# Four dense expert tiles instead of five, with two tiles of the first part gathered early into five row buffers

## The chip, the cores and the metric

The kernel runs on one core of one Trainium2 chip. The metric is the device time of one execution in microseconds. A core has TensorE (PE; its weight loads are listed as PEld), VectorE (DVE), ScalarE (ACT), GpSimd (POOL), SyncE (SP, which issues plain DMAs here) and 16 DMA engines that all queues share.

## The reference

One layer of a decoder trunk for 1024 prompt tokens and 32 sample tokens (8 requests of 4), model width 1024, in float32: a mixing block (dilated window attention in 8 heads beside a gated linear recurrence in 4 heads), a cross attention to 256 memory tokens, a PEER feed-forward block, and a final norm. The feed-forward block is what the change is about. For every token, 8 heads choose 16 of 16384 single-neuron experts:

```python
e = (take_along_axis(i1, ci // 16) * 128 + take_along_axis(i2, ci % 16))   # expert numbers, 8 x 16 per token
g = softmax(sc)
u = peer_u[e]                                      # rows of 1024 floats
a = gelu(einsum('td,thkd->thk', x, u))
y = einsum('thk,thkd->td', g * a, peer_v[e])
```

The outputs are the normed rows of all tokens, the new keys, values and recurrent states, and the memory keys and values.

## The kernel before

**Tiles and parts.** The tokens make nine tiles: 0 to 7 are 128 prompt tokens each, 8 is the 32 sample tokens. Everything up to the choice of experts is done in three parts (`PARTS`, line 24): tiles 0, 1, 2, then 3, 4 and the sample, then 5, 6, 7. A part has a `middle` (projection, attention, recurrence, line 505) and a `tail` (output projection, cross attention, scores of the 128 x 128 product keys, and `select_tile`, line 924, which finds the 16 experts of each head). `run` (line 1211) interleaves generators by weights: the middle of one part beside the tail of the part before (lines 1239 to 1244). The projections use three matmuls for one product (line 202 to 204: high x high, high x low, low x high), since every operand is split into a rounded part and a rest.

**Two ways through the experts.** A tile in `DENSE` (line 25) is computed against all 16384 experts by matmuls. For it `gates` (line 993) first builds a table of gate values, expert by token, out of one-hot comparisons (lines 1013, 1018, or 1021 and 1022 on ACT) and small matmuls (line 1024), and stores it to DRAM (`gtall`, line 1030, 8 MiB for a tile). `LATE` gives for each dense tile how many of four comparisons go to ACT. The gates of the first `NG` dense tiles run beside the second part's tail, the others beside the third part's tail. Then `dense` (line 1034) goes through 128 steps, each with 128 experts: it loads a block of `u` (line 1070) and of `v` (line 1072), 512 KB each, splits both into two halves (lines 170, 171), multiplies all dense tokens with `u` (lines 202 to 204, tile `a`; before in two halves of 320 tokens), applies Gelu (line 1082), multiplies by the gates (line 1084), splits again, and adds the product with `v` (lines 1092 to 1094). `KG = (3, 4)`: three tiles accumulate in PSUM throughout (`y`), the others are added up every fourth step in `yr` and SBUF (`ys`, line 1121).

Any other tile is gathered (`gather_tile`, line 1159): for each of its 128 expert slots (32 for the sample, which is spread over the partitions) an indirect DMA fetches 128 rows of `peer_u`, 512 KB, one row for each token (line 1177, on POOL's queue), and one VectorE instruction forms 128 dot products (line 1184). After Gelu and gates, as many rows of `peer_v` are fetched and added up by line 1195. So a whole tile takes 256 gathers and the sample 64. Each fetch needs a row buffer of 4 KB in every partition: `g_row` (line 1153) has two in the pool `gat`; once `EARLY` = 90 gathers are written down in the program, three in each five come from the pool `more`, which opens in the dense stage, when the selections of the last part are done and `late` is closed (line 1253). The two buffers of `gat` also serve as staging for gates (`BIG`, line 1007). Tile `ha` (the tokens, then the sum), `ix`, `gw` and `dots` exist once, so a tile's loads wait for the tile before.

**Order.** The program is handed to a scheduler that orders each engine's instructions beforehand by a timeline of its own and by the program's order; gathers come last in the program, so they fill gaps. On the chip each queue then runs in that fixed order. The selections of tiles 5, 6, 7 are put off into the dense stage (`picks`, line 703). Gathered are, in this order, the tiles 8, 7, 6, 5 (line 1258), 832 gathers in all. GpSimd writes the descriptors of indirect DMAs into an area of SBUF whose size is an argument of `Bacc` (line 1356; 16384 bytes of each partition if not given).

Of the kernel before, what the change touches and what calls it, by code (L numbers as in the profile page):

```python
# [8 lines left out]
F32 = mybir.dt.float32  # L9
# [11 lines left out]
D = 1024  # L21
EPS = 1e-6
NEG = -1e30
PARTS = ((0, 1, 2), (3, 4, 8), (5, 6, 7))
DENSE = (0, 1, 2, 3, 4)
NG = sum(t in PARTS[0] for t in DENSE)
GT = 16

# [5 lines left out]
VS = 1  # L34
XA = (16, 1)
GA = (10, 1)
EARLY = 90
KG = (3, 4)
VS2 = 1
LATE = (0,0,2,2,2)  # L40
MR = 3
LB = 3
RAW = 1
BIG = 1
W0 = (1,1)
W1 = (2,1,1)
W2 = (2,1,1)
# [18 lines left out]
def _body(tc, nc, ctx, A, O):  # L66
# [24 lines left out]
    def T(p, shape, dt=F32, tag=None, bufs=None):  # L91
        seq[0] += 1
        kw = {} if bufs is None else {"bufs": bufs}
        if p is wk:
            p = wl if tag in LONG else wr if tag == "res" else we
        return p.tile(shape, dt, name=f"{tag}_{seq[0]}", tag=tag, **kw)
# [72 lines left out]
    def split(hi, lo, src):  # L169
        S.copy(hi, src)  # L170
        V.tensor_tensor(lo, src, hi, op=ALU.subtract)  # L171
# [862 lines left out]
    def dense(dv, dn, dps):  # L1034
# [28 lines left out]
        def hidden(i, out):  # L1063
            if i == 0:
                for h in (1, 0):
                    for r in range(4):
                        gate_piece(0, h, r)
            k, h = divmod(i // 4 + 2, 2)
            gate_piece(k, 1 - h, i % 4)
            uhl = load_split(dn, [128, 8, 128], A["uT"][i], "u", 5)  # L1070
            u = [[y[:, 4 * j : 4 * j + 4] for y in uhl] for j in range(2)]
            vhi, vlo = load_split(dv, [128, D], vrow[i], "v", 11)
            ga = T(dv, [128, M], F32, "w", 11)
            whi, wlo = (T(dv, [128, M], F32R, "w", 11) for j in range(2))
            out.extend((whi, wlo, vhi, vlo))
            for h in range(2):
                lo, hi = h * (M // 2), (h + 1) * (M // 2)
                kg, ki = divmod(i + 4 * h, 8)
                ki -= 4 * h if kg == 0 else 0
                pa = T(dps, [128, 512], F32, "a", 6 - 2 * KEEP + 1 if KEEP > 2 else 2)[:, : M // 2]  # L1080
                mm3(pa, u, x, 8, slice(lo, hi))
                S.activation(ga[:, lo:hi], pa, AF.Gelu)  # L1082
                gv = ga[:, lo:hi].rearrange("p (b t) -> p b t", t=GT)
                V.tensor_tensor(gv, gv, gts[kg, h][:, :, ki], op=ALU.mult)  # L1084
                split(whi[:, lo:hi], wlo[:, lo:hi], ga[:, lo:hi])
                yield

        def product(o, t, dh, ws, start, stop):
            sl = slice(t * 128, (t + 1) * 128)
# [11 lines left out]
        for i in range(128):  # L1101
# [9 lines left out]
                del kept[:n]  # L1111

            next(ahead, None)
            keep(KEEP - 1)
            next(ahead, None)
            for t, dh in sums:
                keep(1)
                ds = slice(dh * 512, (dh + 1) * 512)
                o = T(dps, [128, 512], F32, "yr", 1 if KEEP > 2 else 2)
                product(o, t, dh, hist[done[t] :], True, True)  # L1120
                V.tensor_tensor(ys[t - KEEP][:, ds], ys[t - KEEP][:, ds], o, op=ALU.add)  # L1121
                done[t] = done[t] + dh * (i + 1 - done[t])
            keep(len(kept))
            next(ahead, None)
            yield
        for t in range(NDT):
            if t < KEEP:
# [24 lines left out]

    def g_row():
        turns[0] += 1
        if rows_done[0] >= EARLY and turns[0] % (MR + 2) > 1:
            return T(more, [128, D], F32, "row", MR)
        return T(gat, [128, D], F32, "row", 2)

    def gather_tile(t):
        smp = t == 8  # L1160
# [94 lines left out]
        for _ in work:  # L1255
            pass
    fps = pool("fps", space=PSUM)
    for t in [t for part in PARTS for t in sorted(part, reverse=True) if t not in DENSE]:
        gather_tile(t)
    finish_sample()  # L1260

# [102 lines left out]
```

## Time and profile before

| | us |
|---|---|
| median of 3 runs | 3695.17 (3675.76 to 3701.54) |
| span of the profiled execution, which is its own time | 3704.7 |
| PE busy | 3390.1 (92%) |
| DVE busy | 2623.8 (71%) |
| ACT busy | 1401.8 (38%) |
| POOL busy | 1102.0 (30%) |
| packets of plain DMAs, share of 16 engines | 45.1% (568.20 MB) |
| packets of gathers, share of 16 engines | 32.7% (436.26 MB) |

Busy time is the time in which an engine has at least one instruction in work, over the whole span. Matmuls are pipelined, so a busy PE is not PE at its peak. The kernel has stages with different limits: the parts until about 1740 us, the dense stage until about 3625 us, and 80 us in which the last rows are gathered. Views of single stages are therefore read beside the totals. "Idle before" in a group of instructions is the time that the engine stood idle just ahead of them, and the arrow names what ended it.

### The profile page before, as it was taken

What the parts mean: (1) busy time and instruction counts of PE and PEld (TensorE: products, weight loads), DVE (VectorE), ACT (ScalarE), POOL (GpSimd) and SP (SyncE); (2) the same over time, 40 slices, a digit from 0 to 9 for tenths busy, and PEclk for the clock granted to TensorE, in tenths of its full rate; (3) what the DMA queues carried; (4) which work ended last, traced back from release to release, by engine and by line L of the source; (5) the groups of instructions that cost most, each with busy time, mean ns of one, the idle gap of its engine ahead of it and who ended that gap; (6) DMA issues with size and microseconds to landing.
All of it is one profiled execution on the core that took longest, in us unless ns stands there. A gap on an engine that the chain in (4) does not pass through costs nothing.

```text
span 3704.7 us, 53428 instructions
## 1 busy us (share of the span) xinstructions
PE 3390.1 (92%) x19338; PEld 2927.2 (79%) x19338; DVE 2623.8 (71%) x6014; ACT 1401.8 (38%) x2673; POOL 1102.0 (30%) x871
## 2 busy tenths in 40 slices
PE   5999999999999889886889999999999999999991
PEld 4876776677886779776779988998889998899980
DVE  4443333244885777789878868987788987888996
ACT  4544434343444555886332222222222222222220
POOL 0000000000000000011246535654555555555664
PEclk9999999999999889998999999999999999999995
DMA  7667776665656475489679969998898998999997
GB/s 239 227 226 248 235 256 225 204 208 193 204 190 209 151 266 210 175 317 322 226 259 346 346 229 330 346 334 307 309 325 317 347 344 297 330 339 324 340 329 254
DMA packets 408519, 1007.87 MB, mean 272 GB/s; under 512 B 43968, under 2 KB 168896, under 8 KB 406848
## 3 DMA queue, kind: packets, MB, share of 16 engines
q1 hardware_dynamic: 288448, 568.20, 45.1%
q0 software_dynamic: 119808, 436.26, 32.7%
q8 instruction: 152, 2.49, 0.3%
q14 instruction: 111, 0.91, 0.1%
HBM read 866.01 MB, written 138.31 MB: 271 GB/s over the span
## 4 chain that ended last, share of the span: by engine, by line
PE 27%; DMA 10%; issue 7%; DVE 7%; POOL 4%; ACT 1%; SPq 0%; POOLq 0%; DVEq 0%; ACTq 0%
DMA row<-in_peer_v,ix 5%; PE a L204 4%; PE a L202 4%; PE a L203 4%; POOL row L1177 4%; PE y L1094 3%; PE y L1093 2%; PE y L1092 2%; DMA row<-in_peer_u,ix 2%; PE yr L1092 2%; PE yr L1093 2%; PE yr L1094 2%; DMA u<-in_uT 2%; DVE row L1184 2%; DVE ha L1195 1%
## 5 line engine op out<-in xcount | busy, mean ns | idle before, releaser
L1177 POOL DMA_INDIRECT row<-in_peer_u,ix x416 | 526.2, 1265 | 669.2 <-DVE dots L1184 412.5
L1177 POOL DMA_INDIRECT row<-in_peer_v,ix x416 | 546.4, 1314 | 451.4 <-DVE ha L1195 298.7
L202 PE MATMUL a<-xh,u 128*128 128x320 f32 x2048 | 635.8, 310 | 38.2 <-ACT u L170 28.3
L204 PE MATMUL a<-xh,u 128*128 128x320 f32 x2048 | 635.8, 310 | 2.9 <-DVE u L171 2.9
L203 PE MATMUL a<-xl,u 128*128 128x320 f32 x2048 | 635.5, 310 | 0.0
L1195 DVE SCALAR_TENSOR_TENSOR ha<-row,dots,ha 128x1024 f32<-128x1024 f32 x416 | 533.4, 1282 | 77.0 <-DMA row<-in_peer_v,ix 66.4
L1184 DVE CUSTOM_DVE_ANT_0 row<-row,ha 128x1024 f32<-128x1024 f32 x416 | 501.5, 1222 | 119.7 <-DMA row<-in_peer_u,ix 99.6
L211 POOL TENSOR_TENSOR rs_r<-rs_m,mhalf 128x3 f32<-128x3 f32 (+2 forms) x25 | 21.2, 854 | 1381.7 <-DVE rs_m L209 1083.0
L202 PEld LDWEIGHTS a<-xh,u 128*128 128x128 f32 x2048 | 387.6, 189 | 52.0 <-ACT u L170 28.6
L203 PEld LDWEIGHTS a<-xl,u 128*128 128x128 f32 x2048 | 387.3, 189 | 10.2
L204 PEld LDWEIGHTS a<-xh,u 128*128 128x128 f32 x2048 | 387.3, 189 | 3.6 <-DVE u L171 3.3
L202 PE MATMUL z<-zhi,wz 128*128 128x384 f32 (+2 forms) x928 | 329.1, 355 | 25.8 <-ACT zhi L170 10.2
L203 PE MATMUL z<-zlo,wz 128*128 128x384 f32 (+2 forms) x928 | 316.4, 341 | 2.8 <-DVE zlo L171 2.1
L204 PE MATMUL z<-zhi,wz 128*128 128x384 f32 (+2 forms) x928 | 313.2, 338 | 0.0
L1092 PE MATMUL y<-v,w 128*128 128x512 f32 x768 | 300.9, 393 | 12.4 <-ACT w L170 12.4
L170 ACT CAST w<-w 128x320 fp32r<-128x320 f32 x256 | 117.8, 460 | 503.9 <-DVE w L1084 476.9
L1093 PE MATMUL y<-v,w 128*128 128x512 f32 x768 | 301.3, 394 | 0.0
L170 ACT CAST u<-u 128x1024 fp32r<-128x1024 f32 x128 | 134.8, 1053 | 364.0 <-PE a L203 276.7
L1094 PE MATMUL y<-v,w 128*128 128x512 f32 x768 | 253.7, 392 | 6.5 <-DVE w L171 6.5
L1082 ACT ACTIVATE w<-a 128x320 f32<-128x320 f32 x256 | 110.8, 433 | 361.5 <-PE a L204 337.9
L202 PEld LDWEIGHTS z<-zhi,wz 128*128 128x128 f32 x928 | 180.3, 194 | 65.9 <-issue 19.6
L1092 PE MATMUL yr<-v,w 128*128 128x512 f32 x512 | 204.1, 399 | 19.9 <-DVE ys L1121 15.6
(466 smaller groups left out, 6966.0 us busy)
## 6 DMA issues: line engine op xcount, KB each, us to landing
u<-in_uT SPq DMA_DIRECT2D x128, 512.0 KB
v<-in_peer_v SPq DMA_DIRECT2D x128, 512.0 KB
wz<-wd_w_in SPq DMA_DIRECT2D x112, 512.0 KB
gt<-gtall SPq DMA_DIRECT2D x124, 320.0 KB
wd_w_in<-wz SPq DMA_DIRECT2D x56, 512.0 KB
gtall<-sg SPq DMA_DIRECT2D x34, 512.0 KB
wd_w_pq<-wt SPq DMA_DIRECT2D x32, 512.0 KB
wt<-wd_w_pq SPq DMA_DIRECT2D x32, 512.0 KB
```

The source lines that it names most:

```text
L170: S.copy(hi, src)
L202: PE.matmul(out, lhsT=whi, rhs=xhi[:, c, sl], start=c == 0, stop=False)
L203: PE.matmul(out, lhsT=whi, rhs=xlo[:, c, sl], start=False, stop=False)
L204: ins = PE.matmul(out, lhsT=wlo, rhs=xhi[:, c, sl], start=False, stop=c == kc - 1)
L211: G.tensor_tensor(r, m, mhalf[:, :n], op=ALU.pow)
L1082: S.activation(ga[:, lo:hi], pa, AF.Gelu)
L1092: PE.matmul(o, lhsT=wh[:, sl], rhs=vh[:, ds], start=start and q == 0, stop=False)
L1093: PE.matmul(o, lhsT=wh[:, sl], rhs=vl[:, ds], start=False, stop=False)
L1094: PE.matmul(o, lhsT=wl[:, sl], rhs=vh[:, ds], start=False, stop=stop and q == len(ws) - 1)
L1177: G.indirect_dma_start(out=row, out_offset=None, in_=tab, in_offset=bass.IndirectOffsetOnAxis(ap=col(ix, j), axis=0))
L1184: V.tensor_tensor_reduce(row, row, hn, 1.0, 0.0, op0=ALU.mult, op1=ALU.add, accum_out=col(dots, j))
L1195: V.scalar_tensor_tensor(acc, row, col(dots, j), acc, op0=ALU.mult, op1=ALU.add)
```

## The change

The dense tiles become 2, 3, 4 and 5; tiles 0 and 1 are gathered instead of computed densely, tile 5 the other way round. The sample moves from the second part to the third. The gathers go in the order 0, 1, 7, 6, 8, which makes 4 x 256 + 64 = 1088. Five row buffers (`NR`) stand in `gat`, the three of `more` are used beside them from gather 400 on, the gates no longer use them (`BIG`), and the descriptor area shrinks from 16384 to 4096 bytes of each partition, which is the room of three row buffers. With 512 dense tokens a step's first product is done in one piece, in one PSUM bank, and the order of the products in a step changes accordingly. `NG` becomes 1. The selections put off into the dense stage are those of tiles 6, 7 and 8.

```diff
-PARTS = ((0, 1, 2), (3, 4, 8), (5, 6, 7))
-DENSE = (0, 1, 2, 3, 4)
+PARTS = ((0, 1, 2), (3, 4, 5), (6, 7, 8))
+DENSE = (2, 3, 4, 5)
+GATHER = (0, 1, 7, 6, 8)
...
-EARLY = 90
+EARLY = 400
...
-LATE = (0,0,2,2,2)
+LATE = (0, 2, 2, 2)
 MR = 3
+NR = 5
...
-BIG = 1
+BIG = 0
...
+            pa = T(dps, [128, 512], F32, "a", 1)
+            mm3(pa, u, x, 8, slice(0, M))
+            S.activation(ga, pa, AF.Gelu)
             for h in range(2):
-                lo, hi = h * (M // 2), (h + 1) * (M // 2)
                 kg, ki = divmod(i + 4 * h, 8)
                 ki -= 4 * h if kg == 0 else 0
-                pa = T(dps, [128, 512], F32, "a", 6 - 2 * KEEP + 1 if KEEP > 2 else 2)[:, : M // 2]
-                mm3(pa, u, x, 8, slice(lo, hi))
-                S.activation(ga[:, lo:hi], pa, AF.Gelu)
-                gv = ga[:, lo:hi].rearrange("p (b t) -> p b t", t=GT)
+                gv = ga[:, h * (M // 2) : (h + 1) * (M // 2)].rearrange("p (b t) -> p b t", t=GT)
                 V.tensor_tensor(gv, gv, gts[kg, h][:, :, ki], op=ALU.mult)
-                split(whi[:, lo:hi], wlo[:, lo:hi], ga[:, lo:hi])
-                yield
+            split(whi, wlo, ga)
+            yield
...
             next(ahead, None)
-            keep(KEEP - 1)
-            next(ahead, None)
             for t, dh in sums:
-                keep(1)
+                keep(2)
...
             keep(len(kept))
-            next(ahead, None)
             yield
...
-        if rows_done[0] >= EARLY and turns[0] % (MR + 2) > 1:
+        if rows_done[0] >= EARLY and turns[0] % (MR + NR) >= NR:
             return T(more, [128, D], F32, "row", MR)
-        return T(gat, [128, D], F32, "row", 2)
+        return T(gat, [128, D], F32, "row", NR)
...
-    for t in [t for part in PARTS for t in sorted(part, reverse=True) if t not in DENSE]:
+    for t in GATHER:
         gather_tile(t)
...
-    nc = _bacc.Bacc("TRN2", target_bir_lowering=False, num_devices=1)
+    nc = _bacc.Bacc("TRN2", target_bir_lowering=False, num_devices=1, dynamic_dma_scratch_size=4096)
```

## Rows read from the trace of the kernel before

**Rows 1.** The page: the span, the busy time of each engine, and the share of the DMA engines in 40 slices of 92.6 us (a digit for tenths).

```profile
span 3704.7 us, 53428 instructions
PE 3390.1 (92%) x19338; PEld 2927.2 (79%) x19338; DVE 2623.8 (71%) x6014; ACT 1401.8 (38%) x2673; POOL 1102.0 (30%) x871
...
DMA  7667776665656475489679969998898998999997
```

**Rows 2.** Busy time by stage, all instructions. Columns: the stretch in us, its length, then busy us and (number of instructions) of PE, PEld, DVE, ACT and POOL, the granted clock, the DMA share, GB/s.

```profile
0.00:1120.00 1120.00, 1049.63 (x5908) 820.03 (x5909) 527.68 (x1894) 492.34 (x940) 17.99 (x25) 0.98 0.67 222
1120.00:1740.00 620.00, 531.92 (x3444) 476.46 (x3442) 468.00 (x1705) 405.69 (x931) 40.39 (x40) 0.94 0.66 232
1740.00:1760.00 20.00, 0.00 (x0) 0.00 (x0) 19.86 (x121) 4.56 (x4) 1.92 (x2) 0.50 1.03 339
1760.00:3630.00 1870.00, 1804.73 (x9984) 1630.34 (x9984) 1567.58 (x2260) 495.60 (x793) 1010.87 (x778) 0.99 0.89 316
3630.00:3670.00 40.00, 0.00 (x0) 0.00 (x0) 30.00 (x26) 1.37 (x4) 27.54 (x24) 0.50 0.95 348
3670.00:3705.00 35.00, 3.80 (x4) 0.36 (x4) 10.63 (x11) 2.30 (x4) 3.34 (x4) 0.50 0.31 104
```

**Rows 3.** TensorE in the dense stage: one group of instructions between 1900 and 3600 us (count | busy us, mean ns), then four single matmuls of its timeline (start, us).

```profile
L1092 PE MATMUL y<-v,w 128*128 128x512 f32 x710 | 278.7, 393 | 12.4 <-ACT w L170 12.4
...
2422.17 0.30 PE L202 MATMUL a<-xh,u 128*128 128x320 f32 x1
2422.32 0.31 PE L203 MATMUL a<-xl,u 128*128 128x320 f32 x1
...
2426.62 0.39 PE L1092 MATMUL yr<-v,w 128*128 128x512 f32 x1
2426.85 0.39 PE L1093 MATMUL yr<-v,w 128*128 128x512 f32 x1
```

**Rows 4.** Who waited for whom between 1950 and 3600 us: total us, times, longest.

```profile
POOL row L1177 <- DVE dots L1184: 351.9, 195, 16.8
```

**Rows 5.** The gathers alone (line 1177) by stretch: busy POOL time and number of gathers, clock, DMA share, GB/s.

```profile
1120.00:1740.00 620.00, 35.97 (x35) 0.94 0.66 232
...
2000.00:3600.00 1600.00, 885.63 (x686) 1.00 0.91 324
```

**Rows 6.** The stores of the first part's first and third selection in SP's timeline, then the first gather in POOL's.

```profile
1053.27 0.32 SPq L980 DMA_DIRECT2D selD<-c  x1
...
1121.07 0.39 SPq L980 DMA_DIRECT2D selD<-c  x1
...
1559.74 1.18 POOL L1177 DMA_INDIRECT row<-in_peer_u,ix  x1 [88.18 <-ACT zhi L238]
```

**Rows 7.** VectorE's groups over the whole span that the sum uses: line, operation, names and shapes, count | busy us, mean ns | idle before.

```profile
L1195 DVE SCALAR_TENSOR_TENSOR ha<-row,dots,ha 128x1024 f32<-128x1024 f32 x416 | 533.4, 1282 | 77.0 <-DMA row<-in_peer_v,ix 66.4 <-DMA ha<-x2d 6.4
L1184 DVE CUSTOM_DVE_ANT_0 row<-row,ha 128x1024 f32<-128x1024 f32 x416 | 501.5, 1222 | 119.7 <-DMA row<-in_peer_u,ix 99.6 <-DMA ha<-h3d 19.1
...
L171 DVE TENSOR_TENSOR u<-u,u 128x1024 fp32r<-128x1024 f32 x128 | 156.3, 1221 | 62.0 <-ACT u L170 61.4 <-issue 0.4
...
L1018 DVE TENSOR_SCALAR oh<-iota,x_vs 128x128 f32<-128x128 f32 x448 | 128.7, 343 | 2.8 <-DMA x_vs<-selD 2.8
...
L1084 DVE TENSOR_TENSOR w<-w,gt 128x320 f32<-128x320 f32 x256 | 124.4, 486 | 25.8 <-ACT w L1082 20.9 <-issue 4.6
...
L1013 DVE TENSOR_TENSOR raw<-iota,x_vs 128x512 f32<-128x512 f32 x160 | 110.2, 688 | 84.8 <-PE g L1024 73.9 <-DMA x_vs<-selD 3.7 <-PE x L1024 3.6
L1121 DVE TENSOR_TENSOR ys<-ys,yr 128x512 f32<-128x512 f32 x130 | 88.6, 682 | 6.5 <-PE yr L1094 6.0 <-issue 0.4
...
L171 DVE TENSOR_TENSOR wt<-raw,wt 128x512 fp32r<-128x512 f32 x80 | 55.1, 689 | 48.1 <-ACT wt L170 47.1 <-DMA sg<-in_s 0.3
```

**Rows 8.** VectorE's timeline, two instructions of line 1184 one after the other: start, us.

```profile
2530.63 1.22 DVE L1184 CUSTOM_DVE_ANT_0 row<-row,ha 128x1024 f32<-128x1024 f32 x1
...
2531.78 1.22 DVE L1184 CUSTOM_DVE_ANT_0 row<-row,ha 128x1024 f32<-128x1024 f32 x1
```

**Rows 9.** DMA issues of the whole program: tile written <- tensor read, count, KB each.

```profile
u<-in_uT SPq DMA_DIRECT2D x128, 512.0 KB
v<-in_peer_v SPq DMA_DIRECT2D x128, 512.0 KB
gt<-gtall SPq DMA_DIRECT2D x124, 320.0 KB
```

**Rows 10.** Two more stretches with the columns of [rows 2], of different width: most of the time after the parts' matmuls, and the last 180 us before they end.

```profile
1740.00:3677.00 1937.00, 1804.73 (x9984) 1630.34 (x9984) 1622.58 (x2409) 501.52 (x800) 1042.57 (x804) 0.97 0.89 317
1560.00:1740.00 180.00, 148.24 (x955) 140.63 (x954) 163.41 (x597) 146.56 (x346) 36.61 (x36) 0.92 0.89 319
```

**Rows 11.** Two stretches of 20 us with the columns of [rows 2].

```profile
1560.00:1580.00 20.00, 18.50 (x123) 17.14 (x123) 17.52 (x41) 19.86 (x51) 6.78 (x6) 1.00 0.99 352
1580.00:1600.00 20.00, 16.66 (x99) 14.95 (x96) 15.34 (x38) 20.00 (x48) 3.44 (x3) 0.83 1.00 384
```

**Rows 12.** The end of the timeline: the last addition of a gathered row and the last store.

```profile
3677.50 1.28 DVE L1195 SCALAR_TENSOR_TENSOR ha<-row,dots,ha 128x1024 f32<-128x1024 f32 x1 [0.66 <-DMA row<-in_peer_v,ix]
...
3697.79 0.32 SPq L1147 DMA_DIRECT2D out_y_sample<-row  x1
```

**Rows 13.** The page's third part, DMA queues over the whole span: packets, MB, the time that their packets took as a share of 16 engines' span. The gathers are q0.

```profile
q0 software_dynamic: 119808, 436.26, 32.7%
```

## The prediction

> **What bounds the kernel now.** I began with the page: TensorE is busy for 92% of the span, VectorE for 71%, and the DMA digits are 5 to 7 in the first half and 9 in the second [rows 1]. Such an average hides stages, so I cut the span where the parts' matmuls end [rows 2]. Until 1740 us TensorE is busy for most of the time and the DMA engines run at 222 and 232 GB/s, two thirds of their time. From 1760 to 3630 us, the dense stage, three things are nearly full together: TensorE 1804.7 of 1870 us, DMA 0.89 at 316 GB/s, VectorE 84%. From 3630 to 3670 us TensorE does nothing, and the last gathers go at 348 GB/s.
>
> In the dense stage TensorE sets the pace. 710 instructions of line 1092 with 6 in a step are 118.3 steps in 1700 us, 14.37 us a step; a 320-column matmul starts 0.147 us after the one before, a 512-column one 0.23 us [rows 3], so 48 of the first and 30 of the second take 13.9 us, 97% of a step. POOL meanwhile waits for VectorE to give row buffers back, 352 us in all for the u rows alone [rows 4]. So a gather is paced by buffers, 686 in 1600 us or 2.33 us each [rows 5], and goes on past the dense stage.
>
> **TensorE: a gain.** After the change all matmuls of a step have 512 columns: 8 chunks x 3 = 24 for the first product, 4 tiles x 2 halves x 3 = 24 for the second. 48 x 0.23 = 11.0 us, over the measured 97% 11.4 us; 128 steps take 1459 us instead of 128 x 14.37 = 1839. If TensorE alone counted, 380 us would go. It doesn't.
>
> **DMA: the price.** 256 more gathers of 0.524 MB are 134 MB, against 8.4 MB less of gate table written and as much less read (a fifth of 128 reads of 320 KB [rows 9]). From 1740 us to the last row the kernel now moves 1937 us x 317 GB/s = 614 MB [rows 10], with 832 - 35 = 797 gathers in it [rows 5]. After the change it is 614 + 0.524 x (1088 - N - 797) - 8.4 + 3 for a fifth tile's loads, where N is the number of gathers issued before 1740 us. So N and the rate decide.
>
> **N.** The third selection of the first part is stored at 1121 us, while the first gather of all goes out at 1560 us [rows 6]. Tiles 0 and 1 can start at 1121 us, 620 us before the parts end. With two buffers the kernel made 35 gathers in 180 us, 5.1 us each: 620 us would hold 121, the lower bound. The upper one is VectorE's free time. It is busy for 468 us of these 620 [rows 2]; off come 35 u rows of 1.15 us (the spacing of two in a row [rows 8]), 40 us, and the gates: three tiles at 32 x (0.688 + 4 x 0.343) = 66 us and two at 32 x (0.688 + 2 x 0.343) = 44 us become one and three [rows 7], 88 us less; on comes tile 5's full selection for the sample's small one, three quarters of the 34 us between selection stores, 25 us. That leaves 255 us, and a row costs 1.15 us (u) to 1.28 us (v) [rows 7, 8]: 208 at most. The DMA side agrees: 232 x 0.620 = 144 MB there, less 18 of gathers and 8 of gates, are 117 MB; filled to 336 GB/s they leave 91 MB, 174 gathers. In 1560 to 1740 us, with two buffers and the gates running, the rate is 319 already [rows 10]. I take N = 175, nearer the upper end, since five buffers lift what held it.
>
> **The rate after 1740 us.** The rows give 317 GB/s where TensorE sets the pace [rows 10], 348 with gathers alone in five buffers [rows 2], and 352 and 384 in two 20 us stretches with gathers beside stores and loads, the share at 1.0 [rows 11]. The new dense stage asks for more than 317, and from gather 400 on eight buffers stand ready. I take 355, above the five-buffer row and below the mean of 368; the ends are 340 and 368.
>
> A sentence by itself: the Trainium skill, "DMA: Bandwidth & Descriptors", section Bandwidth, says that transfers between HBM and SBUF are bound at about 358 GB/s for a core; the two stretches of 352 and 384 show that this trace goes beyond it for 20 us, and by that figure the sum below would be 3626 us.
>
> **VectorE: nearly full.** After 1740 us it is busy for 1622.6 us [rows 10]. 116 more rows at 1.22 us add 142. A dense step falls from 2 x 1.15 + 4 x 0.41 = 3.94 us (each duration less the 0.07 us by which neighbours overlap [rows 7, 8]) to 2.30 + 0.62 + 2 x 0.37 = 3.66 us, 0.37 being between the 128- and 320-column rows; with half of line 1121's additions gone that is 75 us less. The small selection saves 25. So 1665 us: 89% of the time below, against 84% now. It costs nothing as long as its order leaves few gaps.
>
> **Edits taken at nothing.** The sample in the third part instead of the second moves 96 columns of a tail and 128 of a projection forward, within the 1740 us; cover is the rest of the parts, and 40 us either way are kept for it in the range. The last row (3677.5 us) to the end takes 27 us [rows 12], and again a sum goes to DRAM and back: the same. A fifth gathered tile waits once more for its tokens and its sum, (19.1 + 6.4) / 3 = 8.5 us [rows 7], hidden while dense loads fill the DMA engines. The gates' staging out of the row buffers costs nothing while ACT's copies find two other tiles.
>
> **The sum.** 614 + 0.524 x 116 - 5.4 = 669 MB at 355 GB/s are 1885 us; 1740 + 1885 + 27 = 3652 us, against this execution's 3704.7, which stands 0.26% above the median of 3695. On the median's scale 3642; I say 3640. TensorE would end about 3225 us, and the last 400 us would be gathers alone. The same formula gives the break-even: 669 MB in 1937 us is 345 GB/s. The gain thus hangs on 3% of the DMA rate, not on TensorE's 380 us.
>
> **Rivals.** *No change.* The rate stays at the 348 of the five-buffer stretch, or VectorE's gaps stay as they are: 669 / 348 = 1922, in the end 3689 - 10 = 3680 us; with 340 GB/s 3725. For it: VectorE at 89% and the DMA engines at 0.97 (355 against 348 / 0.95 [rows 2]) at the same time is more than any long stretch shows. Against it: the pace of gathers is now set by buffers, and there will be more.
>
> *Slower: the early rows hold up the parts.* VectorE runs in a fixed order, and a row instruction that stands ahead of a part's instruction keeps it for 1.2 us, or longer if its row has not landed. The place is 1121 to 1740 us, where TensorE is busy for 532 of 620 us and so waits for other engines already [rows 2]. Half an instruction for each of 175 rows, 0.6 us, is 105 us, if each falls on the chain and no more gathers are gained by it: 3745 us. It decides from about 90 us of delay on. For it: VectorE would be at 92% there. Against it: gathers fill gaps by the scheduler's order, and more time before the dense stage also holds more gathers.
>
> *Slower: the early gathers don't come.* With N at 121 or below, (669 + 28) / 348 = 2003, so 3760 us. Against it: the indices lie in DRAM from 1121 us on.
>
> *The smaller descriptor area binds.* Each gather makes 119,808 / 832 = 144 packets, 9 for each DMA engine [rows 13], and no row shows the area filling. Were gathers held to two at a time by it, the 5.1 us above would hold for all 1088, 5550 us from 1121 us on. By the Trainium skill ("DMA: Bandwidth & Descriptors", section SWDGE vs HWDGE vs iDMA, and the 16-byte descriptor of its terms) the rings lie in this area; an estimate from that page is 4096 / 16 = 256 descriptors for an engine, 28 gathers, where eight buffers allow eight.
>
> **How the numbers follow.** A measurement of this kernel can tell about 1%, so faster means below 3658. The forecast has 0.45, with its own range 3555 to 3658 (368 GB/s alone gives 669 / 368 = 1818, so 3575; N = 208 alone 652 / 355 = 1836, so 3593; both 3528, and I stop between); no change 0.27; held-up parts 0.17; late gathers 0.10; the area 0.01. So faster 0.45, same 0.27, slower 0.28. The range 3555 to 3790 takes in the forecast, no change and the slower cases, whose upper end has the 40 us of the moved sample on top.
>
> **What would show it.** Right: the first gather near 1121 us, some 175 before the parts end, the dense stage near 11.4 us a step, TensorE idle for hundreds of us at the end, 350 GB/s or more throughout. No change: the same picture at 340 to 348. Held up: the parts end after 1830 us, VectorE waiting for rows in the stretch from 1121 us. The forecast is wrong at its root if the dense steps stay near 14 us, or if gathers wait where neither buffers nor DMA rate explain it.

## The result, and the profile after

The changed kernel takes 3744.88 us (median of 4 runs, 3739.42 to 3755.34), the kernel before beside it 3698.36 (4 runs). The ratio is 1.0127, 95% interval 1.0088 to 1.0165: slower by 1.3%, where 3640 us and a gain of 1.5% were forecast. The profiled execution took 3747.6 us.

The page of the changed kernel, first the same lines as [rows 1] and then its DMA queues, to be held against [rows 13] and the table of before:

```profile
span 3745.6 us, 45501 instructions
...
PE 3104.0 (83%) x15242; PEld 2484.6 (66%) x15242; DVE 2788.2 (74%) x6047; ACT 1300.9 (35%) x2339; POOL 1478.5 (39%) x1127
...
DMA  7667566547768899778989899999999989989997
...
q1 hardware_dynamic: 267168, 551.69, 42.2%
q0 software_dynamic: 156672, 570.49, 41.5%
```

TensorE has 286 us less to do, as the change intends. The gathers' queue carries 134 MB more, the plain queue 16.5 MB less. The DMA digits stand at 7 to 9 from slice 13 on (about 1120 us), where [rows 1] had 4 to 7 in slices 13 to 17.

Where the time went shows when the span is cut at the changed kernel's own stages. Busy time by stage, with the columns of [rows 2]; the third line is the stretch from the first gathers to the first dense product, the fifth the dense stage:

```profile
0.00:1120.00 1120.00, 1051.32 (x5877) 818.74 (x5878) 520.33 (x1806) 497.82 (x938) 16.33 (x23) 0.99 0.66 220
1120.00:1740.00 620.00, 391.09 (x2041) 325.99 (x2041) 516.12 (x1478) 204.66 (x442) 278.21 (x221) 0.77 0.86 304
1120.00:2047.00 927.00, 579.04 (x3221) 490.81 (x3220) 783.30 (x2234) 379.76 (x863) 389.69 (x317) 0.79 0.88 314
1760.00:3630.00 1870.00, 1598.28 (x7043) 1290.15 (x7042) 1640.74 (x2611) 563.60 (x886) 1109.76 (x825) 0.94 0.94 347
2047.00:3676.00 1629.00, 1468.96 (x6139) 1174.29 (x6140) 1433.09 (x1961) 418.88 (x531) 1040.25 (x759) 0.97 0.95 349
1740.00:3727.00 1987.00, 1657.82 (x7324) 1339.52 (x7323) 1748.55 (x2761) 597.32 (x959) 1183.43 (x883) 0.93 0.94 347
```

Up to 1120 us nothing changed. The parts' last matmul, near 1736 us before, comes at 1989 us, and the first dense matmul (tile `a`) at 2038 us instead of 1764. The first product with `v`, called the first dense product below, comes at 2057 us instead of 1781; the dense stage is counted from some 10 us ahead of it, here 2047. In the old kernel's stretch from 1120 to 1740 us TensorE is busy for 391 us instead of 532, and VectorE for 516 instead of 468. Then the dense stage runs at 349 GB/s to 3676 us, 12.7 us a step. Of the 400 us of gathers alone that were forecast there is almost nothing. The gathers of line 1175 by stretch (busy POOL time and count, clock, DMA share, GB/s, as in [rows 5]):

```profile
1120.00:1740.00 620.00, 268.48 (x215) 0.77 0.86 304
1120.00:2047.00 927.00, 378.37 (x309) 0.79 0.88 314
2047.00:3676.00 1629.00, 1037.97 (x755) 0.97 0.95 349
3676.00:3746.00 70.00, 29.02 (x24) 0.52 0.71 273
```

**One sum says it.** From 1120 us to the last row (about 3727 us) 337 GB/s were moved, 2607 us x 337 = 879 MB. Before, it was 757 MB at 296 GB/s in 2557 us (both from one window each; a table below has them beside those of the experiments). The 122 MB more would have cost nothing at 879 / 2557 = 344 GB/s; 337 were reached. 337 is the mean of 314 before the dense stage and 349 in it. The question for the experiments was what kept the first stretch at 314, and whether 349 could have been more.

VectorE's timeline in that stretch (start, us, line; in brackets the idle time before and what ended it) shows the rows between the steps of the cross attention's softmax, lines 596 (maximum), 597 (scale) and 602 (reciprocal):

```profile
1260.83 0.69 DVE L596 TENSOR_REDUCE c_st<-x 128x2 f32<-128x512 f32 x1
...
1262.37 1.22 DVE L1182 CUSTOM_DVE_ANT_0 row<-row,ha 128x1024 f32<-128x1024 f32 x1 [0.79 <-DMA row<-in_peer_u,ix]
...
1263.52 0.22 DVE L597 TENSOR_SCALAR c_st<-c_st,xs 128x2 f32<-128x2 f32 x1
...
1264.87 1.22 DVE L1182 CUSTOM_DVE_ANT_0 row<-row,ha 128x1024 f32<-128x1024 f32 x1 [1.06 <-DMA row<-in_peer_u,ix]
...
1266.02 0.16 DVE L602 RECIPROCAL c_st<-c_st 128x2 f32<-128x2 f32 x1
```

Line 597 needs only the result of line 596, which took 0.69 us; it starts 2.7 us after the start of that one, behind a row that took 1.22 us and had waited 0.79 us to land. That a row stands there costs the chain, but whether the chain costs the kernel is not seen in such a view.

### The profile page after: what moved, and what is told of

The parts are those of the page before. It is cut to its first block, busy times and chain, and to the rows that moved or that the text cites. A ratio compares the mean times of both kernels' runs of the same rounds, so it can differ in the third digit from the quotient of the medians.

```text
span 3745.6 us, 45501 instructions
## 1 busy us (share of the span) xinstructions
PE 3104.0 (83%) x15242; PEld 2484.6 (66%) x15242; DVE 2788.2 (74%) x6047; ACT 1300.9 (35%) x2339; POOL 1478.5 (39%) x1127
## 5 line engine op out<-in xcount | busy, mean ns | idle before, releaser
L1175 POOL DMA_INDIRECT row<-in_peer_u,ix x544 | 746.1, 1372 | 655.2 <-DVE dots L1182 221.8
L1175 POOL DMA_INDIRECT row<-in_peer_v,ix x544 | 699.3, 1285 | 571.1 <-DVE ha L1193 385.3
L1193 DVE SCALAR_TENSOR_TENSOR ha<-row,dots,ha 128x1024 f32<-128x1024 f32 x544 | 697.6, 1282 | 11.9 <-DMA row<-in_peer_v,ix 3.9
L204 PE MATMUL a<-xh,u 128*128 128x512 f32 x1024 | 411.9, 402 | 75.5 <-ACT u L172 69.4
L206 PE MATMUL a<-xh,u 128*128 128x512 f32 x1024 | 414.0, 404 | 66.7 <-DVE u L173 66.7
L205 PE MATMUL a<-xl,u 128*128 128x512 f32 x1024 | 408.5, 399 | 0.0
L204 PE MATMUL z<-zhi,wz 128*128 128x288 f32 (+3 forms) x928 | 319.7, 345 | 59.3 <-ACT zhi L172 19.4
L205 PE MATMUL z<-zlo,wz 128*128 128x288 f32 (+3 forms) x928 | 308.3, 332 | 3.4 <-DVE zlo L173 3.3
L206 PE MATMUL z<-zhi,wz 128*128 128x288 f32 (+3 forms) x928 | 304.8, 328 | 0.0
L206 PEld LDWEIGHTS a<-xh,u 128*128 128x128 f32 x1024 | 198.7, 194 | 127.2 <-DVE u L173 86.1
L204 PEld LDWEIGHTS a<-xh,u 128*128 128x128 f32 x1024 | 198.5, 194 | 127.1 <-ACT u L172 79.4
L205 PEld LDWEIGHTS a<-xl,u 128*128 128x128 f32 x1024 | 198.1, 193 | 41.7
L204 PE MATMUL y<-thi,wt 128*128 128x384 f32 (+1 forms) x576 | 208.0, 361 | 14.4 <-DVE res L554 5.0
```

The source lines that it names most:

```text
L204: PE.matmul(out, lhsT=whi, rhs=xhi[:, c, sl], start=c == 0, stop=False)
L205: PE.matmul(out, lhsT=whi, rhs=xlo[:, c, sl], start=False, stop=False)
L206: ins = PE.matmul(out, lhsT=wlo, rhs=xhi[:, c, sl], start=False, stop=c == kc - 1)
L1175: G.indirect_dma_start(out=row, out_offset=None, in_=tab, in_offset=bass.IndirectOffsetOnAxis(ap=col(ix, j), axis=0))
L1193: V.scalar_tensor_tensor(acc, row, col(dots, j), acc, op0=ALU.mult, op1=ALU.add)
```

## Experiments

Unless said otherwise each is an edit of the changed kernel, and a time without an interval is that of one execution. The first three share a chip and their runs of before (median 3701.75 us).

### All early gathers taken away: late_gather

```diff
-GATHER = (0, 1, 7, 6, 8)
+GATHER = (7, 6, 8, 0, 1)
```

Tiles 7, 6 and 8, which are selected late, come first, so no gather can start before the dense stage.

> The changed kernel with the gather order 7, 6, 8, 0, 1 in place of 0, 1, 7, 6, 8: tile 7's experts are chosen in the dense stage, so no gather runs beside the parts. Three theories for the first dense matmul, which moved from 1767 to 2047 us. Hold-up (row instructions in VectorE's fixed order keep the parts waiting) and crowding (the early gathers' bytes keep the parts' loads waiting) both expect it back near 1740 to 1780 us. Layout (the sample in the third part, the gates' staging out of the row buffers, three gates late) expects it to stay above 1950 us. For the time: if the DMA engines set it, 1088 gathers after the parts are 761 MB at 352 GB/s, so about 3930 us; if the early gathers cost the parts as much as they save, it stays within 2% of 3745.

Measured: 3941 us. Busy time by stage (columns of [rows 2]), parts, dense stage, gathers alone:

```profile
1120.00:1767.00 647.00, 516.48 (x3276) 454.35 (x3274) 435.20 (x1782) 377.33 (x860) 7.84 (x7) 0.90 0.58 201
1774.00:3221.00 1447.00, 1402.70 (x6095) 1150.99 (x6095) 1240.29 (x1687) 414.99 (x523) 811.33 (x609) 0.99 0.93 337
3221.00:3921.00 700.00, 2.12 (x5) 1.11 (x4) 621.19 (x735) 6.25 (x12) 517.79 (x487) 0.50 0.97 373
```

Without early rows the dense stage begins at 1767 us with the new order of tiles, and its first dense product comes at 1774 us (1781 before): neither the sample's move nor tile 5's place in the second part delays the parts. So the 280 us (1767 to 2047) belong to the 309 early rows, 0.9 us each, for what they fetch and what VectorE does with them together. A dense step takes 1447 / 128 = 11.3 us, with 607 gathers in the stage. And the dense stage that starts 280 us sooner and ends 455 us sooner gives a kernel that is 197 us slower than the changed one: the rows not gathered early are gathered at the end. The DMA engines had stood at 0.58 while the parts ran.

### VectorE's part of the early rows taken away, then the transfers: early_dma_only, early_dve_only

The first cuts VectorE's two instructions for a row to 8 of 1024 columns in tiles 0 and 1 and fetches all of it; the second fetches 16 of 128 partitions there and keeps VectorE's work at full size (its instructions then read the tokens or the sum in place of the row and write into the row, so they still wait for the fetch; those lines are not shown). Both leave sums of tiles 0 and 1 out.

```diff
+            n = 8 if t in (0, 1) else D
-            V.tensor_tensor_reduce(row, row, hn, 1.0, 0.0, op0=ALU.mult, op1=ALU.add, accum_out=col(dots, j))
+            V.tensor_tensor_reduce(row[:, :n], row[:, :n], hn[:, :n], 1.0, 0.0, op0=ALU.mult, op1=ALU.add, accum_out=col(dots, j))
...
-            V.scalar_tensor_tensor(acc, row, col(dots, j), acc, op0=ALU.mult, op1=ALU.add)
+            V.scalar_tensor_tensor(acc[:, :n], row[:, :n], col(dots, j), acc[:, :n], op0=ALU.mult, op1=ALU.add)
```
```diff
+            n = 16 if t in (0, 1) else 128
-            G.indirect_dma_start(out=row, out_offset=None, in_=tab,
-                                 in_offset=bass.IndirectOffsetOnAxis(ap=col(ix, j), axis=0))
+            G.indirect_dma_start(out=row[:n], out_offset=None, in_=tab,
+                                 in_offset=bass.IndirectOffsetOnAxis(ap=col(ix, j)[:n], axis=0))
```

> The changed kernel with VectorE's work on the gathered rows of tiles 0 and 1 cut to 8 of 1024 columns (the rest of their sums is left out); every fetch stays. Hold-up expects the first dense matmul near 1800 us instead of 2047, though more gathers fit beside the parts. Crowding expects it to stay near 2000 us or later, and the whole time within 1% of 3745 us, since no byte less is moved.

> The changed kernel with the fetches of tiles 0 and 1 cut to 16 of 128 partitions (so their sums are left out), 235 MB less; VectorE's instructions keep their full width and still wait for their fetch. Hold-up expects the first dense matmul to stay at 1950 us or later. Crowding expects it near 1800 us. The whole time falls in both, by up to 235 MB / 350 GB/s = 670 us where the DMA engines set it, and by less where VectorE does.

Measured: 3659.8 and 3849.8 us. The first dense product came at 1937 and at 2212 us (changed kernel: 2057). In the first run neither expectation was met: the product came between the two, and the time lies 2.3% below 3745. In the second, hold-up's 2212 came, but the whole time rose by 105 us where both accounts expected a fall. First the transfers alone (columns of [rows 2]; the parts, then the dense stage):

```profile
1120.00:1930.00 810.00, 548.56 (x3209) 470.43 (x3208) 467.28 (x2192) 373.61 (x858) 299.80 (x302) 0.84 0.94 349
1930.00:3619.00 1689.00, 1486.90 (x6117) 1183.11 (x6118) 1252.62 (x2012) 416.45 (x532) 1006.80 (x794) 0.95 0.95 348
```

Then VectorE's work alone (the parts, and the end of the dense stage):

```profile
1120.00:2205.00 1085.00, 575.07 (x3178) 491.77 (x3177) 974.16 (x2488) 381.82 (x862) 555.41 (x479) 0.72 0.47 149
3583.00:3825.00 242.00, 241.76 (x1066) 199.52 (x1064) 89.39 (x124) 66.99 (x86) 0.56 (x1) 1.00 0.35 113
```

With the transfers alone the parts run at the pace of the DMA engines: their own 647 us x 201 GB/s = 130 MB and 294 gathers of 0.524 MB are 284 MB, which at 349 GB/s are 814 us, and 810 were measured. With VectorE's work alone the DMA share is 0.47, and the parts still last 1085 us; VectorE is busy for 90% of them, 435 us of its own work, as in late_gather's first line, and 470 rows in 539 us, 1.15 us each. The delay for each early row is 0.55 us in the first run ((1930 - 1767) / 294) and 0.93 us in the second (438 / 470), as much as in the changed kernel (0.91). So VectorE's work on the early rows is the longer of the two delays, and the transfers are a second one that comes close behind it. The first run answers the main question too: with the same bytes, at 348 GB/s from 1120 us to the last row, the time is 3660 us, 85 us below the changed kernel. Its cut covers all 512 rows of tiles 0 and 1, and 218 of them are gathered in the dense stage; the rate there is 348 GB/s, where the changed kernel has 349, so the gain lies in the stretch before it. The 35 GB/s that the changed kernel lacks over 927 us are 32 MB, 93 us at 349 GB/s.

The second run shows where bytes stop deciding. It moves 235 MB less and is slower: its dense stage begins 155 us later, its last gather goes out at 3567 us, and from 3583 to 3825 us TensorE alone sets the pace (241.76 of 242 us, DMA share 0.35).

Where in the stretch they are lost is seen in 1500 to 1660 us, when selections (`top16` and what follows it, lines 920 to 973) and rows share VectorE. Changed kernel:

```profile
1120.00:1500.00 380.00, 265.32 (x1406) 237.65 (x1406) 306.40 (x920) 100.69 (x202) 180.91 (x143) 0.79 0.90 321
1500.00:1660.00 160.00, 67.29 (x306) 45.02 (x304) 145.79 (x438) 31.80 (x60) 72.43 (x56) 0.66 0.74 258
1660.00:2047.00 387.00, 246.43 (x1513) 208.14 (x1511) 331.10 (x878) 247.27 (x601) 136.36 (x119) 0.84 0.92 330
```

Against 349 GB/s the three lines lack 11, 15 and 7 MB: in the middle one, a sixth of the stretch, VectorE is busy for 91%, DMA falls to 0.74 and nearly half of the loss arises.

### VectorE's load cut elsewhere in the stretch: first_gates_act

```diff
-LATE = (0, 2, 2, 2)
+LATE = (4, 2, 2, 2)
```

Timed against before on the same chip (3704.35 us).

> The changed kernel with all four comparisons of the first dense tile's gates on ScalarE instead of VectorE: 128 instructions of 0.343 us, 44 us of VectorE's time, leave the stretch from 1120 to 2047 us, and ScalarE, busy for 41% of it, takes 128 x 0.91 = 116 us more. Theory (VectorE's load in that stretch, with the fetched rows in it, is what the 105 us between the forecast and the result come from): the first dense product comes 25 to 60 us earlier than 2057 us, the stretch's DMA rate rises above 314 GB/s, and the whole takes 3690 to 3725 us. Rival (the rows' place in the cross attention's chain costs the time, whatever else VectorE does; free time elsewhere in the stretch is only filled by more rows): first product within 20 us of 2057, the whole 3735 to 3755 us.

Measured: 3745.15 us, ratio to before 1.0096 (1.0066 to 1.0126), an interval that overlaps the changed kernel's. The first dense product came at 2029 us, 28 us sooner, as the theory said; the time is the one that the rival gave. Three stretches, the middle one with the selections (columns of [rows 2]):

```profile
1120.00:2047.00 927.00, 581.98 (x3287) 493.80 (x3286) 772.94 (x2203) 448.54 (x1078) 382.55 (x317) 0.80 0.88 316
1500.00:1700.00 200.00, 91.48 (x442) 59.54 (x440) 175.33 (x461) 81.46 (x187) 81.95 (x65) 0.71 0.79 268
2047.00:3676.00 1629.00, 1457.51 (x5993) 1162.15 (x5991) 1414.40 (x1881) 405.97 (x518) 1036.63 (x758) 0.95 0.95 347
```

The same 309 gathers lie before 2047 us, and the rates are those of the changed kernel within 3 GB/s. From 1500 to 1700 us VectorE is as busy as in the changed kernel (175.33 against 175.36 us of 200), so the time was freed where the DMA engines had work anyway (of the changed kernel's 292 comparisons on VectorE between 1120 and 2047 us 10 lie between 1500 and 1660). The rival's own reason, that it is the place in the cross attention's chain, isn't shown by this; what is shown is that the dense stage can begin 28 us sooner without an effect on the time that these runs can tell: its steps then take 13.1 us instead of 12.7. Where the DMA engines are this full (0.95 in the dense stage), bytes over time decide, not when the dense stage begins. My theory as written, that any 44 us off VectorE in that stretch would do, fell.

### Fewer early rows, fewer late buffers: two_early, five_in_dense

These two ran beside each other (before 3702.62 us). The first has two early buffers and six late ones, the second five throughout.

```diff
-EARLY = 400
+EARLY = 130
...
-MR = 3
-NR = 5
+MR = 6
+NR = 2
```
```diff
-EARLY = 400
+EARLY = 2000
```

> The changed kernel with two early row buffers and six late ones (eight from gather 130 on) instead of five and three. Early gathers go at about 5 us each, some 130 beside the parts instead of 309. VectorE account (the stretch from 1120 us to the dense stage is its busy time without gathers, 435 us, plus 1.19 us for a row, over 0.85): (435 + 155) / 0.85 = 694, first dense product near 1820 us instead of 2057. DMA account ((130 + 0.524 N) MB at 349 GB/s): no delay, 1775 us. The whole time: a row beyond the hundredth costs the parts 1.4 us and a row after the dense stage 1.49, so the VectorE account expects within 1.5% of 3745 though the dense stage starts 240 us earlier; if the delay of the parts were the loss itself, about 3510.

> The changed kernel with the five early buffers alone, the three late ones never used. The parts should stay as they are (first dense product near 2057 us). If the eight buffers are what stretches a dense step from 11.3 us (no gathers early, five buffers) to 12.7 us, a step falls to 11.3 to 11.6 us, and about 170 gathers are left for after the dense stage: 2047 + 1460 + 170 x 1.49 + 27 = 3790 us. If it is something else (the later start, the order), a step stays near 12.7 us.

Measured: 3867.8 us and 3875.2 us; both expectations of the time missed: the first lies 67 us above the end of its 1.5%, the second 85 us above 3790. The first dense product of two_early came at 1898 us, later than both accounts said (1820 and 1775), 0.93 us for each of its 133 early rows. The step of five_in_dense was met: 11.3 us. It shows in its dense stage, and in the gathers alone behind it (columns of [rows 2]):

```profile
2060.00:3501.00 1441.00, 1403.84 (x6116) 1150.69 (x6117) 1222.16 (x1741) 418.96 (x525) 787.83 (x589) 0.99 0.92 331
3501.00:3847.00 346.00, 1.16 (x6) 0.60 (x4) 249.45 (x239) 5.04 (x10) 243.72 (x193) 0.51 0.87 302
```

I had held the longer step of eight buffers for a loss. It is the opposite: the step of 12.7 us carries more gathers (755 in 128 steps, against 587 here), and the rows left over cost 1.8 us each alone, with five buffers. The stretches from 1120 us to the last row, for all of these kernels, from their windows (the dense stage begins some 10 us ahead of the first dense product; for the kernel before, the second and third column go to 1740 us):

| kernel | gathers before the dense stage | GB/s before it | dense step, us | from 1120 us to the last row, us | GB/s | MB |
|---|---|---|---|---|---|---|
| before | 35 | 232 | 14.4 | 2557 | 296 | 757 |
| late_gather | 0 | 201 | 11.3 | 2801 | 314 | 880 |
| two_early | 133 | 258 | 13.2 | 2728 | 322 | 878 |
| five_in_dense | 308 | 316 | 11.3 | 2737 | 322 | 881 |
| changed kernel | 309 | 314 | 12.7 | 2607 | 337 | 879 |
| first_gates_act | 300 | 318 | 13.1 | 2607 | 336 | 876 |
| early_dma_only | 294 | 349 | 13.2 | 2516 | 348 | 876 |

With four dense tiles the bytes are 876 to 881 MB whatever the order, and the time is those bytes over the mean rate. The dense step alone does not tell it. Among the versions that compute everything the changed kernel and first_gates_act fill the DMA engines best.

### What stretches a dense step: dense_dve_only, dense_dma_only

The same two cuts, now for tiles 7 and 6, which are gathered inside the dense stage.

```diff
+            n = 16 if t in (7, 6) else 128
```
```diff
+            n = 8 if t in (7, 6) else D
```

> The changed kernel, with the fetches of tiles 7 and 6 (the two tiles gathered inside the dense stage) cut to 16 of 128 partitions, so that their rows are mostly not moved; VectorE's work on all 512 rows stays whole. Tiles 0 and 1 as they are, so the first dense product should come near 2050 us as in the changed kernel. Theory A (the DMA engines stretch a dense step from 11.3 to 12.7 us): a step takes 11.3 to 11.6 us, the dense stage ends near 3500 us, the whole near 3540 to 3600. Theory B (VectorE's row instructions between the dense ones stretch it): a step stays at 12.4 us or more, as it was in the run with the early tiles' fetches cut, and the dense stage ends after 3630 us.

> The changed kernel, with VectorE's two instructions for each row of tiles 7 and 6 cut to 8 of 1024 columns; all their rows are fetched in full. The first dense product should come near 2050 us. Theory A (the DMA engines stretch a dense step): a step stays at 12.5 us or more, since 1.6 MB of loads and some 4.6 gathers of 0.524 MB in a step are 4.0 MB, 11.5 us at 349 GB/s already, and buffers freed sooner bring more gathers, not fewer. The gathers then end well before the dense stage and the whole takes 3640 to 3700 us. Theory B (VectorE stretches it): a step takes 11.3 to 11.7 us, the dense stage ends near 3500 to 3550 us, and the remaining gathers follow: about 3600 to 3650 us in all.

Measured: 3755.8 and 3789.2 us, both no faster than the changed kernel, with steps of 13.1 and 13.4 us. The step of the first is the one that theory B gave and that of the second the one that theory A gave, while both times lie above what theory A gave, and the second above theory B's 3650 too; neither theory holds alone. The last gather went out at 3515 and 3695 us, ahead of the end of the dense stage at 3730 and 3764. In the stretch from 2600 to 3100 us, first with VectorE's work alone:

```profile
2600.00:3100.00 500.00, 412.19 (x1642) 325.94 (x1642) 483.65 (x665) 106.76 (x137) 344.46 (x304) 0.91 0.46 131
```

With the transfers alone:

```profile
2600.00:3100.00 500.00, 431.62 (x1730) 343.71 (x1729) 184.35 (x581) 112.40 (x145) 260.65 (x256) 0.93 0.97 365
```

And the changed kernel:

```profile
2600.00:3100.00 500.00, 448.77 (x1865) 357.77 (x1864) 444.64 (x572) 127.16 (x161) 342.04 (x242) 0.96 0.97 360
```

In the first VectorE is busy for 97%, in the second the DMA share is 0.97. Counting gathers and Gelus (one for each step) in these 500 us gives 303 / 34 = 8.9 rows in a step, 255 / 36 = 7.1, and 241 / 39 = 6.2 in the changed kernel; late_gather has 221 / 43 = 5.1. How many rows stand between two steps is written into VectorE's order beforehand, and it changed with the cuts, so these runs don't hold all else equal. They do give the load at each pace. A step loads two blocks of 0.524 MB and 0.262 MB of gates, 1.31 MB; with 6.2 rows it moves 4.56 MB, which at the 360 GB/s of that stretch are 12.7 us; with 7.1 rows at 365 GB/s, 13.8 us (500 / 36 = 13.9); with 5.1, 3.98 MB in 11.6 us, 343 GB/s (348 by late_gather's window, where TensorE is busy for 476 of the 500 us). At 8.9 rows it is VectorE: 484 us in 34 steps, 14.2 of 14.7 us. By these shares the changed kernel's dense stage runs close to the DMA engines' limit (0.97), and VectorE lies not far behind it (89% in that stretch). That this is why taking one of them away didn't help is argued, not shown, since the order of the rows changed with each cut.

### The descriptor area and row buffers in the kernel before

Four edits of the kernel before, all with the small area: the area alone (before_small_area), its room as three more early buffers (before_eight_rows: five and three), one early and two late (before_three_five), and all late (before_six_late: two and six).

```diff
-    nc = _bacc.Bacc("TRN2", target_bir_lowering=False, num_devices=1)
+    nc = _bacc.Bacc("TRN2", target_bir_lowering=False, num_devices=1, dynamic_dma_scratch_size=4096)
```
```diff
+NR = 5
...
-        if rows_done[0] >= EARLY and turns[0] % (MR + 2) > 1:
+        if rows_done[0] >= EARLY and turns[0] % (MR + NR) >= NR:
...
-        return T(gat, [128, D], F32, "row", 2)
+        return T(gat, [128, D], F32, "row", NR)
```

> The kernel before with the descriptor area of 4096 bytes and nothing else. No theory gives it a part: 3695 to 3705 us, no change. If the area binds, slower by 1% or more.

> The kernel before with the small descriptor area and five row buffers beside the three late ones, five dense tiles, nothing gathered earlier. If the gathers of the kernel before were paced by their five buffers, they now end with the dense stage: its 80 us of gathers alone shrink to about 30, so 3650 us. If the dense steps pay for the faster gathers (14.37 us a step becomes 14.7 or more), the time stays at 3695. If the small descriptor area holds gathers back, it is slower than 3735.

> The kernel before with the small descriptor area and, of the three more row buffers that it makes room for, one in the pool that is there from the start (three) and two in the pool of the dense stage (five). With all three in the early pool the time was 3679 us, with all three in the late pool 3713. Theory (VectorE and the DMA engines are both nearly full, and rows early in the parts relieve the dense stage only where VectorE has free time): it lands between the two, 3680 to 3710 us, as the third early buffer brings fewer early rows than five do. Rival (eight buffers in all are what counts, wherever they are): 3675 to 3685 us.

> The kernel before with the room of the smaller descriptor area given to the late row buffers: two early buffers as before, six late ones instead of three. By the VectorE account the parts keep their length (first dense product near 1781 us, where five early buffers had 1810), the dense stage keeps its 1855 us, and the gathers end with it: 3645 us. If it is the faster gathers beside the dense steps that cost, the time stays at 3680 or above.

Measured, as the ratio to before on the same chip: 0.9993 (0.998 to 1.0005); 0.9952 (0.9928 to 0.9977), 3679.24 us; 0.9985 (0.996 to 1.001), 3694.39 us; 1.0025 (1.001 to 1.0041), 3712.92 us. So the area alone, the split into three and five, and the six late ones came as their no-change, theory and second case said (0.25% slower in the last); before_eight_rows lies between its first two cases, with the step at 14.4 us. The area costs nothing that can be measured. The buffers help only where they let rows in early, and late ones cost a little: in the profiled execution with six of them, the slowest of 12, a dense step takes 15.0 us instead of 14.4, and the dense stage ends at 3711 us; its last gather came at 3616. The best of the four, in its dense stage (columns of [rows 2]) and in what comes behind its last gather:

```profile
1810.00:3653.00 1843.00, 1790.86 (x9909) 1614.33 (x9908) 1559.18 (x2262) 493.97 (x791) 1038.49 (x773) 0.99 0.88 318
...
3550.00:3660.00 110.00, 104.57 (x546) 89.65 (x544) 50.55 (x73) 31.68 (x53) 4.01 (x6) 0.95 0.35 116
```

It makes 64 gathers before 1800 us instead of 35 before 1740, ends its last gather at 3544 us instead of 3671, and is then bound by TensorE to the end. It is the one version that beats both kernels, with five dense tiles: by 0.5% the one, and by 1.7% the other (0.9952 / 1.0127 = 0.983, each measured against before).

## Why the prediction was wrong

The forecast's sum was 1740 + 669 MB / 355 GB/s + 27. In its own form the result is 1740 + 690 / 0.347 + 20 = 3748. So it missed by 59 us through the bytes (21 MB at 355), by 45 us through the rate, and the tail gave 7 back. Either alone would have taken nearly all of the gain (3704 us with the bytes, 3688 with the rate, where the execution of before took 3704.7); the slowdown took both.

- **TensorE: right, and of no use.** Steps of 11.3 us (late_gather, five_in_dense) against 11.4 forecast. In the changed kernel a step takes 12.7, with 6.2 rows in it and the DMA engines near their limit. The end of the dense stage at 3225 us, with 400 us of gathers alone, didn't come: it ended at 3676.
- **N at no cost: the step that failed.** 215 gathers went out before 1740 us, more than the 175 forecast and even a little over the upper bound of 208. But the sum had the parts end at 1740 unchanged, because VectorE had 255 us free. In these parts that time was not free for rows with a place in a fixed order: VectorE got no fuller than 83% on average (516 of 620 us), the 309 rows that stood in the order before the dense stage moved its start by 280 us, and 42 MB of the parts' own traffic slid behind 1740 us (690 MB, where 669 - 40 x 0.524 = 648 were left by the count of gathers). early_dma_only shows VectorE's share in it: without its work on these rows 662 MB instead of 690 are left at 1740 us, they move at 349 GB/s in 1896 us, and the time is 3660 us, within 1% of the forecast. Even there the parts did not end at 1740: the transfers alone delayed the dense stage by 163 us.
- **The free time itself was counted too high.** `LATE` of the kernel before leaves four comparisons on VectorE for two tiles and two for three; the prediction had it the other way round. So the gates free 66 us instead of 88, VectorE has 233 us free instead of 255, and the bound is 191 rows. This made no difference to N, which came out above either bound.
- **The rate of 355: too high.** 347 from 1740 us to the last row: 335 up to 2047 us, in the held-up parts, and 349 in the dense stage. The rival took 348. The 20 us stretches [rows 11] misled me towards the upper end: over 500 us at a time the dense stage reaches 360, but not for its whole length. The row that I read as 348 with gathers alone in five buffers was not that. The queues of the kernel before from 3630 to 3670 us (packets, MB, share) have 274 GB/s of gathers and 74 of the dense stage's last plain transfers:

```profile
q0 software_dynamic: 3002, 10.94, 75.4%
q1 hardware_dynamic: 823, 2.97, 19.3%
```

- **VectorE at 89% after 1740 us**: 1748.55 of 1987 us, 88%. That the share came out is luck: its busy time was 84 us above the 1665 forecast, and the stretch was longer in about the same proportion. Of its share of the blame after 2047 us only this is shown: it and the DMA engines are nearly full together.
- **Held-up parts: the rival that came true**, and its 3745 us too, but that figure by luck. It had 0.6 us for each of 175 rows, 105 us; it was 0.9 us for each of 309, 280 us, most of it paid back because the longer parts take in 134 more rows than were forecast. Its sign, VectorE waiting for rows, was wrong. From 1120 to 2040 us (total us, times, longest) it waited little for u rows; mostly it was working (783 of 927 us), and others waited for it:

```profile
DVE row L1182 <- DMA row<-in_peer_u,ix: 31.5, 39, 2.5
```

- **No change**: right on the rate, wrong in letting N stand. **Early gathers don't come**: the first left at 1133 us. **The area**: 0.9993, in the kernel before.
- **The sample, tile 5, the gates' staging at nothing**: right within 7 us, as late_gather's first dense product comes at 1774 us without a single early row, and at 1781 before.

Left open: why six late buffers stretch the old kernel's step to 15.0 us, and how much of 349 against 360 GB/s is VectorE's; what keeps the dense stage's rate under the 355 forecast is not shown. That rows could be placed so that the selections don't meet them wasn't tried.

## What to carry to other kernels

When a change trades one engine's work for transfers, sum the bytes from the first point at which the paths differ to the end, and ask for the mean rate that breaks even; here 344 GB/s over 2557 us, and the kernel stood at 337. The sum tells the time only while the transfers are what is left at the end: early_dve_only moved 235 MB less and was 105 us slower. Work that fills gaps on an engine with a fixed order can lengthen the chain beside it by most of its own duration (here 0.9 us for a row of 1.2 us, with VectorE at 84 to 90%), so free time in a busy stretch should be discounted. A stage that starts or ends sooner need not be worth anything: late_gather's dense stage ended 455 us sooner, and the kernel was 197 us slower.

## What the runs showed of the hardware

- Behind the dense stage, with almost nothing but gathers, eight buffers ran at 373 GB/s over 700 us with a share of 0.97 (late_gather), five at 302 over 346 us with 0.87 (five_in_dense); beside the dense loads 349. The Trainium skill, "Perfetto Trace Analysis", section Engine Utilization, notes that 358 GB/s is a core's share while both cores of a pair are active, and that a single one can pull more. Here, with one core at work, 373 over 700 us agrees with it, so the bound that the prediction cites did not hold for this kernel, and not for 20 us alone.
- TensorE's granted clock fell where it idled behind VectorE: from 1500 to 1660 us it was busy for 67 of 160 us at a mean of 0.66, between its levels of 1.2 and 2.4 GHz. Over the parts the clock was 0.79, and the same matmuls kept it busy for 579 us, against 516 at 0.90 in late_gather (3221 and 3276 of them recorded).
- A quarter of the descriptor area made no difference within 0.2% with five row buffers and gathers of 144 packets each (before_small_area); with eight buffers no run has the full area beside it.
